# Squares of an RMS norm partly added on GpSimd instead of summed on TensorE: a decoder trunk in fp32

## The chip, the cores and the metric

One core of one Trainium2 chip. The metric is the device time of one launch in microseconds (us), the median of the runs shown.

## The reference, cut to what matters

The kernel computes one inference step of a two-layer decoder trunk for a prompt of 1024 tokens (with 16 learned tokens ahead) and 8 single sample tokens, 1048 token columns in all, in fp32. Layer 0 mixes by retention and a gated linear recurrence, layer 1 by RWKV-7; a gated FFN with a short convolution follows each, and a last norm gives y.

```python
def rms_norm(x, g):
    y = x * lax.rsqrt(jnp.mean(x * x, axis=-1, keepdims=True) + EPS)
    return y * g

x = x + mixer0(rms_norm(x, norm_mix_g[0]))
x = x + conv_ffn(rms_norm(x, norm_ffn_g[0]))
x = x + mixer1(rms_norm(x, norm_mix_g[1]))
x = x + conv_ffn(rms_norm(x, norm_ffn_g[1]))
y = rms_norm(x, norm_final_g)
```

The change touches the mean of x * x in these five norms, over 1024 features.

## The kernel before, in words

Features lie on the partitions and tokens along the free axis. `x` is kept in SBUF as 8 feature tiles (m = 0 to 7) of 128 x 1048, and the tokens are worked in three blocks (`TBS`: 350, 350 and 348 columns). An fp32 product is made of three float32r passes on TensorE (`mm`, L335 to L337): each operand is split in a high part by an ACT copy (L323) and a low part by a VectorE subtraction (L324), both in `split`. Weights come in blocks of 128 x 1024 and are split in the same way.

The program is written in the order in which it is to run, and each engine works off its own instructions in that order. `Weave` runs the dense products as steps and puts side work between them when its share of the time comes up.

An RMS norm of one token block has these parts:

- `norm_sq` (L417): ACT squares one feature tile (L419), into a scratch tile `tmp` (a pool of five) or, at the start, a slot `T`.
- `norm_acc` (L423): TensorE multiplies the squares by a matrix of ones in plain fp32 (L429), so that the sum over the partitions comes out on all of them; eight such sums per block add up in one PSUM bank, `nrm`. With `keep=2` the last two squares stay queued until the next call.
- `norm_scale` (L446 and `rsqrt`, L434 to L437): VectorE takes the mean from PSUM, ACT looks up the inverse root, three VectorE instructions refine it into `rs`.
- `norm_steps`: for each feature tile the emission of h: x times gain times `rs` on VectorE, and the split of the result. The scaling is L479 for the first mixer and both FFNs, L1098 (`norm_emit`) for the RWKV mixer, and L2042 (`fin`) for the last one, where the result is not split but stored.

The norm stands at five places. At the **start**, `layer0` squares and sums block 0 directly; then the squares of the next block alternate with the emission of the block before (`order`, L918 to L925), and its eight sums follow the emission. At the **end of layer 0** and of **both FFNs**, `norm_after` is called behind each step of the product group that completes x (`group_steps` with `tb_outer`: token blocks outside, feature tiles inside). Such a step is six products (two K-tiles), x += product on VectorE (L405, one input in PSUM), a Square, and a sum. After m = 7 of a block its norm is queued as side work behind the steps of the next block. At the end of the recurrence, **before the second FFN**, `finish` (L1934) sums block 0 beside the last output steps and then squares and sums blocks 1 and 2.

Two things hang on the emission after the first FFN. Its first call of `norm_emit` allocates eight slots and starts eight loads of the shift rows (128 x 8) from GpSimd's DMA queue (L1094), and ACT and VectorE split each of them. GpSimd also starts the loads and stores of the FFN's states (L2064, L2066).

Of the kernel before, what the change touches and what calls it, by code (L numbers as in the profile page):

```python
# [29 lines left out]
# ---------------------------------------------------------------- vectors  # L30
# [14 lines left out]
def constants():  # L45
    """Tables that depend on shapes alone."""
# [41 lines left out]
# ---------------------------------------------------------------- host layout  # L88
def cols(v):
    """(..., n*128) -> (128, ..., n): features on partitions."""  # L90
    v = np.asarray(v)
    r = v.reshape(v.shape[:-1] + (v.shape[-1] // 128, 128))
    return np.moveaxis(r, -1, 0)


def wblocks(w):
    """(K, M) -> (M/128, 128, K/128 * 128): one block per 128 output features."""
    k, m = w.shape
    return w.reshape(k // 128, 128, m // 128, 128).transpose(2, 1, 0, 3).reshape(m // 128, 128, k)


def gblocks(w, groups):
    """(K, 1024) cut along K in groups of g tiles -> blocks that hold 8, 4 or 2 output tiles x g K-tiles."""
    out = []
    k0 = 0
    for g in groups:
        a = w[k0 * 128:(k0 + g) * 128].reshape(g, 128, 8, 128).transpose(2, 1, 0, 3)
        n = (8, 4, 2, 2)[g - 1]
        for i in range(0, 8, n):
            out.append(a[i:i + n].transpose(1, 0, 2, 3).reshape(128, n * g * 128))  # L110
        k0 += g
    return out
# [80 lines left out]
# where the parts of a head pair's arithmetic stand beside the next products, in sixths of a 128-wide output tile  # L193
# [9 lines left out]
# K-tiles between stages of which GpSimd takes the lower part  # L203
POOL = (1, 3, 4)

# and of which it takes the mix
MIXP = (4,)

# shares of PE time given to the parts beside the products
L0K = {"start": 0.088, "rope": 0.5, "tr": 1.05, "ret0": 1.312, "ret": 0.35, "lru0": 2.42, "lru1": 2.2, "lru2": 2.2,  # L210
       "lru3": 1.76, "conv": 3.221, "group": 0.748, "wait": 3.6, "norm": 0.845, "norm1": 0.28}
# ---------------------------------------------------------------- device
# [4 lines left out]
class Weave:  # L217
    """Emits dense steps and, between them, side steps as their share of the time comes up."""
# [42 lines left out]

class Prog:
    def __init__(self, tc, io):
        self.tc, self.nc, self.io = tc, tc.nc, io
        self.wq, self.loaded, self.ready = [], [], []
        self.spare, self.nbanks = None, 0
        self.normed, self.sqs, self.nps = set(), [], {}

    # ---- weights: loads two blocks ahead, exact split into two float32r parts one block ahead
# [33 lines left out]
    def scale_w(self, t, kind, j):  # L303
        """Scales a block of w1 | a1 (or g1) by mix (j = 0) or 1 - mix along K."""
# [21 lines left out]
    # ---- one PSUM bank of a product: sum over k of W[k]^T X[k], in three exact float32r passes  # L326
# [21 lines left out]
    # steps of one 128-wide output tile, each token block in so many parts; evac(tb, psum view, c0, c1).  # L348
    # late: the weights of the next tile are not split before this one; pre: they are once its products are out
# [18 lines left out]
    # two tiles side by side at the start of a phase, each token block as soon as its norm is there  # L368
# [6 lines left out]
    # the same tile with the K-tiles outermost: each K-tile of X is done with as early as can be  # L375
# [15 lines left out]
    # steps of x += W^T y over a group of g K-tiles; a weight block holds 8/g output tiles  # L391
# [23 lines left out]
    # ---- RMS norm in parts: squares as the tiles of x become final, the scale per token block, then h  # L415
    def norm_sq(self, m, tb, room=None):
        c0, c1 = TBS[tb]  # L417
        sq = self.tmp(c1 - c0) if room is None else room[:, :c1 - c0]
        self.nc.scalar.activation(out=sq, in_=self.x[:, m, c0:c1], func=AF.Square)  # L419
        self.sqs.append((m, tb, sq))  # L420

    # adds up squares over the features, all but the last few queued
# [8 lines left out]
    def rsqrt(self, y, v, t):  # L431
        """y = v ** -0.5: table value and one Newton step; t is scratch like v."""
# [17 lines left out]
    # emit(m, tb, rs) may return its second half, which then follows the next one's first  # L450
# [14 lines left out]
    # called after each step of the product that completes x: adds up the squares and queues the norm  # L465
# [36 lines left out]
class Layer0:  # L502
# [10 lines left out]
    # ---- retention, head h: q and k with the rotary applied (features on partitions), v by tokens  # L513
# [41 lines left out]
    def dense_ga(self, h, e):  # L555
        """Gate columns of head h: y = silu(g) * (normed o * gain), split as it comes."""
# [14 lines left out]
    # ---- retention core of head h: stages of a chunk one step apart.  # L571
    # All of a chunk's outputs carry gamma^-(c+1), which the group norm takes out again (its eps carries the square).
    def ret_steps(self, h):
# [57 lines left out]
        # chunk 0: the sample rows, each with its own state, and the 16 leading prompt rows  # L631
# [68 lines left out]
        # the stages of a chunk are one step apart  # L700
# [8 lines left out]
    # ---- RG-LRU, one block of 128 features  # L709
# [21 lines left out]
    def lru_steps(self, g):  # L731
        """a = exp(-y) with y = 8 softplus(-lam) r, and sqrt(1 - a^2) = sqrt(t) (1 + a) with t = tanh(y / 2)."""
# [148 lines left out]
def softplus_neg(p, nc, pool):  # L881
    """lamc = 4 softplus(-lam) = 4 (max(-lam, 0) + ln(1 + exp(-|lam|)))."""
# [13 lines left out]
def layer0(p, pool, H, wv):  # L896
# [3 lines left out]
    # norm of the input: the squares of a token block beside the norm of the one before  # L900
# [8 lines left out]
    def sums():  # L909
        for m in range(8):  # L910
            p.norm_sq(m, 0)
            p.norm_acc()
            if m == 5:
                p.prefetch(1)
# [11 lines left out]
    # the tensor engine's clock only rises with use  # L926
# [34 lines left out]
class FFN:  # L961
    """x += W_down^T (gelu(conv(W_ug^T h)) * (W_uv^T h)); f tiles are used in groups of four."""
# [85 lines left out]
class Layer1A:  # L1048
    """RWKV-7, everything up to the recurrence: h, projections, per-chunk decays; results go to scratch in DRAM.

    The decay products inside a chunk of 64 tokens are taken relative to the chunk's 32nd token."""
# [24 lines left out]
    # second-stage low-rank weights have their own queue  # L1076
# [10 lines left out]
    # ---- h of the layer, with the row before each group in front: emitted as x becomes final  # L1087
# [16 lines left out]
    def mix_a(self, n, k, t, pool=False):  # L1104
        """t = (1 - mix_n) h + mix_n h_prev, K-tile k."""
# [11 lines left out]
    def weave(self, steps, side):  # L1117
        """Runs dense steps; side entries (position in sixths of the tile, f) come after the steps before them."""
# [9 lines left out]
    def transition(self, tile, n, temps, side):  # L1128
        """The last tile of a stage with the K-tiles outermost, each K-tile of X replaced by the next stage's after it."""
# [12 lines left out]
    # ---- first stage of the low-rank paths, with the token shift taken after the product:  # L1142
    # evacuation of the product with the shifted weights (j = 0) and with the others (j = 1)
# [36 lines left out]
    def evac_to(self, dst, smp, **act):  # L1180
        """prompt columns to dst[0:1040], sample columns to smp"""
# [13 lines left out]
    # ---- r, and the decays of head pair m relative to the middle of the chunk  # L1195
# [41 lines left out]
    # ---- keys and the per-chunk factors of head pair m  # L1237
# [83 lines left out]
    # sums over the 64 channels of each of two heads, tokens on the partitions: column 2 i + head for the block at HBLK[i]  # L1321
# [7 lines left out]
    # and from there back to all channels of the heads  # L1329
# [16 lines left out]
    def rsq(self, w, y, t):  # L1346
        """t = w ** -0.5 (table value and one Newton step); y is scratch."""
# [6 lines left out]
    def rs_mul(self, v, w, y, t):  # L1354
        """v *= w ** -0.5; y and t are scratch."""
# [11 lines left out]
    # ---- values: by tokens for the recurrence; the gate and the bonus folded into out = yn G1 + G2  # L1367
# [53 lines left out]
    # ---- inverse of I - A on the 32x32 diagonal blocks: forward substitution, one block per partition  # L1421
# [31 lines left out]
    # ---- sample rows: one step of the recurrence each, heads' value rows on the partitions  # L1453
    def samp_pre(self):
# [30 lines left out]
        # rows by sample, then to scratch as (vector, head, sample, key)  # L1485
# [160 lines left out]
class Layer1B:  # L1646
    """RWKV-7 recurrence in chunks of 64 tokens, heads in pairs on the partitions, and the output projection.

    With A = b~ scores, per chunk: U = (I - A_ab)^-1 (a~ S0 + A_ak V), Y = r~ S0 + A_rb U + A_rk V,
    S1 = scale (S0 + b^T U + k^T V). Even heads keep (U, V) rows stacked as U on partitions 0-63 and V on  # L1650
    64-127, odd heads the other way round, so that products over both run on all 128 rows."""
# [45 lines left out]
    # ---- what does not depend on the state: scores, transposed factors, the inverse's lower block  # L1697
# [64 lines left out]
    # ---- the chain  # L1762
# [72 lines left out]
    # ---- group norm over the 64 values of a head, then out = yn G1 + G2  # L1835
# [50 lines left out]
    def run(self, pool):  # L1886
# [15 lines left out]
        for i, u in enumerate(units):  # L1902
# [22 lines left out]
            # a block of tokens is complete one unit after its last chunk  # L1925
# [7 lines left out]
    # the last block of tokens, with the sums for the next norm beside it  # L1933
# [21 lines left out]
def build(tc, io):  # L1955
    nc = tc.nc
    with ExitStack() as ctx:
# [8 lines left out]
        p.rst = pool("rst", 1)  # L1966
        xt = p.x = const.tile([128, 8, T], F32, name="x")
# [5 lines left out]
        with tc.manual_schedule():  # L1973
# [17 lines left out]
            with ExitStack() as cx1:  # L1991
# [10 lines left out]
                with ExitStack() as cx2:  # L2002
# [11 lines left out]
                    # the recurrence's first loads take the place of the layer's X  # L2014
# [70 lines left out]
```

## Time and profile before

| | us |
|---|---|
| median of 3 runs | 3528.8 |
| the runs | 3524.53, 3528.80, 3534.92 |
| span of the profiled execution | 3527.9 |
| TensorE busy | 3305.9 (94%) |
| VectorE busy | 1800.3 (51%) |
| ACT busy | 1241.4 (35%) |
| GpSimd busy | 361.6 (10%) |

The profile is of one execution. Its span runs from the first to the last instruction; no time of its own beside the span is given for it, so it is set against the three runs. Busy times are sums over the whole span, and engines overlap. In rows of the timeline the first number is the start of an instruction (or of a run of like ones) in us from the span's start, the second its length; in brackets is the time its engine sat idle before it, and what ended that. L429 is line 429 of the kernel before.

### The profile page before, as it was taken

Reading aid. Unit: us, or ns where it says so; the run is one execution under the profiler, and the core shown is the slowest. Engines: PE = TensorE matmul, PEld = TensorE weight load, DVE = VectorE, ACT = ScalarE, POOL = GpSimd, SP = SyncE. Lnnn points to the kernel's source line nnn. Section 1 sums busy time; section 2 is a strip of 40 time slices with the busy share of each in tenths; the row PEclk is TensorE's granted clock in tenths of the full one; section 3 lists DMA queues with packets and bytes.
Section 4 is the critical chain, followed back from the end, with each engine's and each line's share of the span. In section 5 each row is a group of like instructions: output and inputs, shape, how many; then the busy total and the mean of one; then the engine's idle time right before and its main releaser. Section 6 shows DMA issues by size and latency. Waiting matters only on the chain.

```text
span 3527.9 us, 55814 instructions
## 1 busy us (share of the span) xinstructions
PE 3305.9 (94%) x23480; PEld 3123.5 (89%) x23480; DVE 1800.3 (51%) x2860; ACT 1241.4 (35%) x2214; POOL 361.6 (10%) x650
## 2 busy tenths in 40 slices
PE   8999999998999999998978978788889999999998
PEld 7999999997999999997978878566767999999997
DVE  4444445556433333334765658677885533333334
ACT  4222224555322212123674444344445312212122
POOL 0110110000000000000111236111210000000000
PEclk9999999999999999999999989678999999999999
DMA  4111211111111111111356768845543111111111
GB/s 134 62 56 60 74 40 46 46 47 34 42 43 48 48 48 42 42 53 48 118 169 169 176 172 232 219 119 143 152 129 96 37 49 46 45 49 42 48 48 64
DMA packets 303066, 294.33 MB, mean 83 GB/s; under 512 B 233056, under 2 KB 248704, under 8 KB 300640
## 3 DMA queue, kind: packets, MB, share of 16 engines
q1 hardware_dynamic: 294368, 262.95, 25.6%
q0 software_dynamic: 8448, 27.82, 2.5%
q8 instruction: 185, 3.03, 0.4%
q14 instruction: 65, 0.53, 0.1%
HBM read 218.95 MB, written 67.47 MB: 81 GB/s over the span
## 4 chain that ended last, share of the span: by engine, by line
PE 29%; DVE 12%; DMA 4%; ACT 3%; issue 3%; SPq 1%; POOL 1%; DVEq 0%; POOLq 0%; ACTq 0%
PE d L337 8%; PE d L335 8%; PE d L336 8%; DVE pr L1439 2%; DVE mt L1441 1%; PE hs L1325 1%; DVE xsl L324 1%; DMA x<-d_pp 1%; DVE wl L324 1%; DMA kq<-d_kq 1%; PE nrm L429 1%; DMA at<-d_ab 1%; DVE x L1213 1%; DVE T L1439 0%; ACT x L1188 0%
## 5 line engine op out<-in xcount | busy, mean ns | idle before, releaser
L335 PE MATMUL d<-xsh,wh 128*128 128x350 f32 (+1 forms) x3656 | 1207.6, 330 | 11.5 <-ACT xsh L323 7.7
L337 PE MATMUL d<-xsl,wh 128*128 128x350 f32 (+1 forms) x3656 | 1193.6, 326 | 5.2 <-DVE xsl L324 5.1
L336 PE MATMUL d<-xsh,wl 128*128 128x350 f32 (+1 forms) x3656 | 1188.0, 325 | 4.4 <-DVE wl L324 4.4
L335 PEld LDWEIGHTS d<-xsh,wh 128*128 128x128 f32 x3656 | 696.2, 190 | 23.2 <-ACT xsh L323 9.3
L337 PEld LDWEIGHTS d<-xsl,wh 128*128 128x128 f32 x3656 | 694.6, 190 | 16.0 <-DVE xsl L324 14.7
L336 PEld LDWEIGHTS d<-xsh,wl 128*128 128x128 f32 x3656 | 696.9, 191 | 7.1 <-DVE wl L324 5.2
L335 PE MATMUL d<-T,wh 128*128 128x350 f32 (+1 forms) x1380 | 463.7, 336 | 15.8 <-DVE x L405 8.9
L324 DVE TENSOR_TENSOR wl<-wst,wh 128x1024 fp32r<-128x1024 f32 x248 | 303.1, 1223 | 320.3 <-ACT wh L323 320.3
L336 PE MATMUL d<-T,wl 128*128 128x350 f32 (+1 forms) x1380 | 445.2, 323 | 2.5 <-DVE wl L324 2.5
L337 PE MATMUL d<-T,wh 128*128 128x350 f32 (+1 forms) x1380 | 445.3, 323 | 1.4 <-DVE T L324 1.4
L323 ACT ACTIVATE wh<-wst 128x1024 fp32r<-128x1024 f32 x248 | 260.7, 1051 | 509.2 <-PE d L337 387.8
L405 DVE TENSOR_TENSOR x<-d,x 128x350 f32<-128x350 f32 (+1 forms) x450 | 230.3, 520 | 322.2 <-PE d L337 322.1
L991 DVE SCALAR_TENSOR_TENSOR T<-T,vec 128x1064 f32<-128x1064 f32 x88 | 116.8, 1327 | 398.2 <-ACT T L989 396.6
L335 PEld LDWEIGHTS d<-T,wh 128*128 128x128 f32 x1380 | 260.0, 188 | 28.2 <-DVE x L405 10.2
L336 PEld LDWEIGHTS d<-T,wl 128*128 128x128 f32 x1380 | 260.1, 188 | 9.9 <-DVE wl L324 3.2
L337 PEld LDWEIGHTS d<-T,wh 128*128 128x128 f32 x1380 | 260.2, 189 | 2.2 <-DVE T L324 2.2
L323 ACT ACTIVATE T<-T 128x1048 fp32r<-128x1048 f32 (+2 forms) x77 | 69.2, 899 | 288.1 <-DVE T L1004 241.2
L985 POOL TENSOR_SCALAR fcout<-T 128x2 f32<-128x2 f32 x44 | 11.2, 254 | 1515.1 <-ACT T L983 1515.1
L983 ACT ACTIVATE T<-d 128x350 f32<-128x350 f32 (+1 forms) x88 | 40.5, 461 | 269.6 <-PE d L337 269.6
L324 DVE TENSOR_TENSOR T<-T 128x1048 fp32r<-128x1048 f32 (+2 forms) x77 | 78.9, 1024 | 76.7 <-ACT T L323 76.7
L1004 DVE TENSOR_TENSOR T<-T,d 128x350 f32<-128x350 f32 x88 | 45.2, 515 | 120.5 <-PE d L337 120.4
L1439 DVE TENSOR_TENSOR pr<-mt,at 128x1 f32<-128x1 f32 (+45 forms) x124 | 93.9, 757 | 19.1 <-DMA at<-d_ab 13.5
(412 smaller groups left out, 4261.4 us busy)
## 6 DMA issues: line engine op xcount, KB each, us to landing
wst<-in_w_up SPq DMA_DIRECT2D x88, 512.0 KB, 3.2
wst<-in_w_down SPq DMA_DIRECT2D x44, 512.0 KB, 3.6
wst<-in_w_in SPq DMA_DIRECT2D x40, 512.0 KB, 3.2
kq<-d_kq SPq DMA_DIRECT2D x17, 1024.0 KB, 6.7
wst<-in_w_o SPq DMA_DIRECT2D x32, 512.0 KB, 4.0
T<-d_sv SPq DMA_DIRECT2D x80, 128.0 KB, 3.8
d_kq<-x SPq DMA_DIRECT2D x16, 544.0 KB, 4.4
d_kq<-x SPq DMA_DIRECT2D x32, 272.0 KB, 5.4
```

The source lines that it names most:

```text
L323: self.nc.scalar.activation(out=h, in_=src, func=AF.Copy)
L324: (eng or self.nc.vector).tensor_tensor(out=l, in0=src, in1=h.bitcast(F32), op=OP.subtract)
L335: mm(ps, lhsT=h, rhs=a, start=start and j == 0, stop=False)
L336: mm(ps, lhsT=l, rhs=a, start=False, stop=False)
L337: mm(ps, lhsT=h, rhs=b, start=False, stop=stop and j == n - 1)
L405: self.nc.vector.tensor_tensor(out=xv, in0=ps, in1=xv, op=OP.add)
L429: self.nc.tensor.matmul(self.nps[tb][:, :n], lhsT=self.ones, rhs=sq, start=m == 0, stop=m == 7)
L983: nc.scalar.activation(out=ub[:, 18 + c0:18 + c1], in_=ps, func=AF.Copy)
L991: nc.vector.scalar_tensor_tensor(out=c, in0=ub[:, j:1064 + j], scalar=w[j], in1=c, op0=OP.mult, op1=OP.add)
L1004: nc.vector.tensor_tensor(out=st["f"][:, c0:c1], in0=c[:, 16 + c0:16 + c1], in1=ps, op=OP.mult)
L1213: nc.vector.tensor_tensor_scan(L, self.rst, s, 0.0, OP.mult, OP.add)
L1439: nc.vector.tensor_tensor(out=pr, in0=mt[:, 0:t, 0:t], in1=at[:, 0:t, t].unsqueeze(1).to_broadcast([n, t, t]), op=OP.mult)
```

## The change

`norm_sq` now writes the square of tile m = 0 into a buffer of its own, `nac` (a new pool `nsp` with one buffer of 128 x 350), and GpSimd adds the squares of m = 1 to 5 onto it. After m = 5 `nac` is queued for TensorE in the place of those six, so that TensorE has three sums per block: `nac`, m = 6 and m = 7. Block 0 of the start (`direct=True`) is as before; the other 14 norms of a block are changed. The squares on ACT and everything on VectorE are the same. Lines behind the new code are up to 15 numbers higher (L429 is L444, L1094 is L1109, L335 is L338; the add is L431).

```diff
+NPOOL = 5
...
-    def norm_sq(self, m, tb, room=None):
+    def norm_sq(self, m, tb, room=None, direct=False):
         c0, c1 = TBS[tb]
-        sq = self.tmp(c1 - c0) if room is None else room[:, :c1 - c0]
+        n = c1 - c0
+        if m == 0 and not direct:
+            sq = self.nac[tb] = self.nsp.tile([128, 350], F32, tag="nac", name="nac")[:, :n]
+        else:
+            sq = self.tmp(n) if room is None else room[:, :n]
         self.nc.scalar.activation(out=sq, in_=self.x[:, m, c0:c1], func=AF.Square)
-        self.sqs.append((m, tb, sq))
+        if not direct and m <= NPOOL:
+            acc = self.nac[tb]
+            if m:
+                self.nc.gpsimd.tensor_tensor(out=acc, in0=acc, in1=sq, op=OP.add)
+            if m == NPOOL:
+                self.sqs.append((0, tb, self.nac.pop(tb)))
+        else:
+            self.sqs.append((m, tb, sq))
...
         for m in range(8):
-            p.norm_sq(m, 0)
+            p.norm_sq(m, 0, direct=True)
             p.norm_acc()
...
         p.rst = pool("rst", 1)
+        p.nsp = pool("nsp", 1)
```

What this does to the order of instructions on an engine is seen at three places.

GpSimd at the end of the first FFN, before (`fcout` is the FFN's state to be stored, `T` the slots of h with the shift rows):

```order
L985 TENSOR_SCALAR fcout<-T 128x2
L986 TENSOR_SCALAR fcout<-T 128x16
L1094 DMA T<-in_st_shift 128x8 x8
L2066 DMA out_fconv<-fcout 128x396
L1064 MEMSET T 128x1088
```

and after:

```order
L1000 TENSOR_SCALAR fcout<-T 128x2
L1001 TENSOR_SCALAR fcout<-T 128x16
L431 TENSOR_TENSOR nac<-nac,tmp 128x350 x8
L1109 DMA T<-in_st_shift 128x8 x8
L431 TENSOR_TENSOR nac<-nac,tmp 128x350 x2
L431 TENSOR_TENSOR nac<-nac,tmp 128x348 x5
L2082 DMA out_fconv<-fcout 128x396
```

The eight loads of the shift rows now stand behind the five adds of the first block and three of the second, and the store of the state behind all 15.

TensorE at the start of layer 0, before, where the first product tile of block 0 ends:

```order
L335 MATMUL d<-xsh,wh 128x350
L336 MATMUL d<-xsh,wl 128x350
L337 MATMUL d<-xsl,wh 128x350
L429 MATMUL nrm<-T,ones 128x350 x8
L335 MATMUL d<-xsh,wh 128x350
```

and after:

```order
L338 MATMUL d<-xsh,wh 128x350
L339 MATMUL d<-xsh,wl 128x350
L340 MATMUL d<-xsl,wh 128x350
L444 MATMUL nrm<-nac,ones 128x350
L444 MATMUL nrm<-T,ones 128x350 x2
L338 MATMUL d<-xsh,wh 128x350
```

Eight sums of the second block have become three, at the same place.

TensorE in the last product group of layer 0, before, around a sum of the first block:

```order
L335 MATMUL rs<-T,wh 128x350
L336 MATMUL rs<-T,wl 128x350
L337 MATMUL rs<-T,wh 128x350
L429 MATMUL nrm<-tmp,ones 128x350
L335 MATMUL d<-T,wh 128x350
L336 MATMUL d<-T,wl 128x350
L337 MATMUL d<-T,wh 128x350
```

and after, where the first sum of that block now stands:

```order
L338 MATMUL rs<-T,wh 128x350
L339 MATMUL rs<-T,wl 128x350
L340 MATMUL rs<-T,wh 128x350
L444 MATMUL nrm<-nac,ones 128x350
L338 MATMUL d<-T,wh 128x350
L339 MATMUL d<-T,wl 128x350
L340 MATMUL d<-T,wh 128x350
```

Before, each step of six products is followed by a sum; now eight steps run without one, then comes that of `nac`, and the other two follow three steps later, ahead of the block's scale.

## Rows read from the trace of the kernel before

**Rows 1.** The page: busy time, share of the span and instructions of each engine

```profile
PE 3305.9 (94%) x23480; PEld 3123.5 (89%) x23480; DVE 1800.3 (51%) x2860; ACT 1241.4 (35%) x2214; POOL 361.6 (10%) x650
```

**Rows 2.** Windows: stretch, length, then PE, PEld, DVE, ACT, POOL busy, PEclk, DMA

```profile
10.00:60.00 50.00, 42.88 (x186) 32.44 (x187) 32.39 (x67) 29.96 (x64) 0.00 (x0) 0.93 0.30 106
...
1620.00:1675.00 55.00, 45.20 (x215) 37.08 (x216) 33.34 (x68) 22.09 (x49) 0.00 (x0) 0.97 0.14 47
...
3465.00:3527.00 62.00, 46.24 (x239) 38.80 (x237) 35.44 (x68) 18.69 (x32) 0.00 (x0) 0.93 0.20 70
```

**Rows 3.** Timeline of TensorE in layer 0's last group, and the chain before the second FFN

```profile
842.40 0.75 PE L429 MATMUL nrm<-tmp,ones 128*128 128x350 f32 x2
...
843.95 0.75 PE L429 MATMUL nrm<-tmp,ones 128*128 128x350 f32 x2
...
2716.46 8.24 PE nrm L429 x28
```

**Rows 4.** Timeline of GpSimd, operations with two inputs in SBUF

```profile
1822.58 2.46 POOL L324 TENSOR_TENSOR xsl<-x,xsh 128x1048 fp32r<-128x1048 f32 x1 [16.16 <-ACT xsh L323]
...
2141.25 1.27 POOL L1520 TENSOR_TENSOR T<-T 128x512 f32<-128x512 f32 x1 [4.20 <-DVE T L1518]
```

**Rows 5.** Timeline of VectorE beside GpSimd, at 1718 to 1727 and at 2141

```profile
1718.66 1.29 DVE L1115 SCALAR_TENSOR_TENSOR x<-T,vec,x 128x1039 f32<-128x1039 f32 x1
...
1720.97 4.87 POOL L324 TENSOR_TENSOR xsl<-T,xsh 128x1048 fp32r<-128x1048 f32 x2 [2.26 <-PE d L337]
...
1721.03 2.42 DVE L1114 SCALAR_TENSOR_TENSOR x<-T,vec,x 128x8 f32<-128x8 f32 x1
1723.38 3.57 DVE L1115 SCALAR_TENSOR_TENSOR x<-T,vec,x 128x1039 f32<-128x1039 f32 x1
1726.87 0.22 DVE L1114 SCALAR_TENSOR_TENSOR x<-T,vec,x 128x8 f32<-128x8 f32 x1
...
2141.80 0.48 DVE L1385 TENSOR_TENSOR x<-hp,T 128x320 f32<-128x320 f32 x1
```

**Rows 6.** Timeline of the start, 22 to 46

```profile
22.54 0.58 DVE L479 SCALAR_TENSOR_TENSOR tmp<-x,vec,rs 128x350 f32<-128x350 f32 x1
...
23.47 0.57 DVE L479 SCALAR_TENSOR_TENSOR tmp<-x,vec,rs 128x350 f32<-128x350 f32 x1
...
29.16 4.87 PE L429 MATMUL nrm<-T,ones 128*128 128x350 f32 x16
...
34.08 0.52 DVE L446 TENSOR_SCALAR tmp<-nrm 128x350 f32<-128x350 f32 x1 [3.58 <-PE nrm L429]
...
45.03 0.59 PE L335 MATMUL d<-xsh,wh 128*128 128x350 f32 x1
```

**Rows 7.** Timeline of VectorE at the end of layer 0

```profile
850.80 0.51 DVE L446 TENSOR_SCALAR tmp<-nrm 128x350 f32<-128x350 f32 x1
...
857.26 0.52 DVE L324 TENSOR_TENSOR xsl<-tmp,xsh 128x350 fp32r<-128x350 f32 x1 [0.52 <-ACT xsh L323]
```

**Rows 8.** The shift rows: timeline of GpSimd and ACT, and the DMA issues

```profile
1606.79 4.28 POOL L1094 DMA_DIRECT2D T<-in_st_shift  x8
...
T<-in_st_shift POOLq DMA_DIRECT2D x8, 4.0 KB, 1.9
...
1645.02 0.88 ACT L323 ACTIVATE xsh<-T 128x8 fp32r<-128x8 f32 x8
```

**Rows 9.** Timeline of ACT in `finish`, before the second FFN

```profile
2717.14 8.07 ACT L419 ACTIVATE tmp<-x 128x350 f32<-128x350 f32 x14 [2.03 <-PE nrm L429]
2725.12 1.04 ACT L323 ACTIVATE wh<-wst 128x1024 fp32r<-128x1024 f32 x1
```

**Rows 10.** Timeline of VectorE at the end of the program

```profile
3497.47 0.52 DVE L405 TENSOR_TENSOR x<-d,x 128x350 f32<-128x350 f32 x1
...
3510.10 0.51 DVE L446 TENSOR_SCALAR tmp<-nrm 128x350 f32<-128x350 f32 x1
```

**Rows 11.** Windows, columns as in rows 2, before the second FFN

```profile
2732.00:2736.00 4.00, 4.00 (x14) 3.48 (x14) 4.00 (x10) 1.99 (x4) 0.00 (x0) 0.50 0.00 0
```

More of the change, by code (lines that the diff above doesn't have):

```diff
@@ L266, in __init__ @@
         self.spare, self.nbanks = None, 0
-        self.normed, self.sqs, self.nps = set(), [], {}
+        self.normed, self.sqs, self.nps, self.nac = set(), [], {}, {}
     def load_next(self):
```

## The prediction

> **What bounds the kernel now.** I read the page's busy times first: TensorE is busy 94% of the span [rows 1]. That is a mean. So I next read the five places where the changed norm runs, in the view of windows: at the start TensorE is busy 42.88 of 50 us, after the first FFN 45.20 of 55, at the end 46.24 of 62, and its granted clock there is 0.93 to 0.97 [rows 2]. TensorE therefore has holes exactly where its sums go. Then the timeline, for prices and for the engine that ends each hole.
>
> An RMS norm makes a chain: sums on TensorE, scale on VectorE (L446), rsqrt, then eight pairs on VectorE (scaling by L479, L1098 or L2042, and the subtraction of `split`), and only then the next products. Where this chain ends last, TensorE time saved beside it is worth nothing.
>
> **What TensorE is rid of.** Of the 120 sums, 70 go (five in each of 14 blocks). In a product group a sum and its six products take 1.55 us (842.40 to 843.95); in the chain of waits 14 sums (28 records) take 8.24 us, 0.59 each [rows 3]. So a step without its sum takes 0.97 us, and 70 x 0.59 = 41 us of TensorE work go. That is the ceiling; the parts below say how little of it lies on the path.
>
> **What GpSimd gets.** 70 adds of 128x350, both inputs in SBUF. No row of before has one. The nearest are adds or subtractions of 512 elements, 1.27 us, and of 1048 elements, 2.46 us [rows 4]: 2.2 ns an element, so about 0.92 us at 350, with a little for the semaphore 0.94; the ends are 0.82 (2.46 in proportion, with no fixed part) and 1.27 us. The Trainium skill (GPSIMD Engine Reference, section 3.1 on elementwise work) times an add of 2048 fp32 elements at 4497 ns, in proportion an estimate of 0.77 us at 350; by it the sum below would be about 3 us smaller.
>
> **What an add does to VectorE.** This term decides. A VectorE instruction with two SBUF inputs takes 1.29 us alone (L1115). Under two GpSimd subtractions that last 4.87 us together, the 8-element L1114 took 2.42 us, where the next one takes 0.22, and L1115 took 3.57 us: each stood until a GpSimd instruction had ended. An operation with one input in PSUM, inside a GpSimd instruction at 2141, took 0.48 us as ever [rows 5]. So x += product (L405) and L446 read PSUM and are free; the scalings, the subtractions and two of the rsqrt's steps have two SBUF inputs and stand for up to a whole add. The Trainium skill (SBUF — State Buffer, "Who interferes with whom") says the same of a VectorE instruction with two SBUF inputs beside a GpSimd one that reads SBUF: whoever starts first holds the shared port pair for its whole instruction. The trace agrees, with 3.57 against 1.29 us, and the rule speaks against this change. Ends: an add costs VectorE nothing, or 0.94 us whole.
>
> **Start (two blocks).** VectorE emits its pairs back to back, 0.93 us a pair (22.54 to 23.47), while ACT squares the next block [rows 6]. Five adds in each of the two emissions cost 5 x 0.94 = 4.7 us each. In the first, eight sums of 4.87 us become three of 1.83, so L446 (34.08) comes 4.7 - 3.0 = 1.7 later. In the second nothing is gained: its sums already stood beside the emission. TensorE's restart at 45.03 moves with it: **+6.4 us**. With adds that cost VectorE nothing it would be -3.0.
>
> **End of layer 0.** The first block's steps are paced by TensorE, so its L446 (850.80) comes earlier by most of 5 x 0.59 = 2.95, say 2.4. From there VectorE's chain paces: a subtraction waits 0.52 us for ACT's half of the split [rows 7], and half of an add fits in that wait. Three adds fall into each emission: 2 x 3 x 0.5 = +3.0. The sum of `nac` stands in TensorE's queue at step m = 7, behind the last add: +0.9. Together **+1.5** (-2.4 to +5).
>
> **End of the first FFN.** The same -2.4, +0.9 and, since VectorE is less loaded [rows 2], +2.4 for the adds. But here a queue is passed. The eight loads of the shift rows (L1094) are issued by GpSimd at 1606.79, 38 us before ACT splits them at 1645.02; they take 4.28 us to issue and 1.9 to land [rows 8]. In the change they stand behind eight adds, the last of which needs the Square of m = 3 in the second block, and that comes at about the time of the split. ACT would then wait for the end of that add, seven more issues (7 x 0.535) and 1.9 us: +5.9 us, with everything queued behind it on ACT, the next Squares and splits. TensorE's cover for that is gone already, since VectorE's chain ends last here. **+6.8** (-2.4 to +9).
>
> **Before the second FFN** (`finish`). Five sums fewer before the last product end (-2.95), but then ACT's Squares, 14 in 8.07 us until 2725.12 [rows 9], are paced by adds through five buffers at about 1.0 us each, and the first Square of a block waits for TensorE's sum of the one `nac` buffer. The weight split behind them comes at about the same time: **0** (-2.9 to +2.5).
>
> **End.** -2.4 up to the first L446. From there to the second, 3497.47 to 3510.10, are 12.6 us [rows 10]; without sums ten steps would take 9.7, and three adds 2.8 more: nothing gained. **-2.4** (-3.5 to 0).
>
> **Clock.** After a hole before the second FFN the granted clock was 0.50, the lower level, for 4 us of full work [rows 11]: 2 us lost, some 2.5 with its edges. The start and the first FFN's end have longer holes in the change; I take one such drop, **+2.5** (0 to 5).
>
> **Sum:** 6.4 + 1.5 + 6.8 + 0 - 2.4 + 2.5 = +14.8 us on the profiled span of 3527.9, thus 3542.7. That span lies 0.9 us below the median of the three runs (3528.8), which vary by more; so 3543 us. About 0.3%, 10.6 us, is what can be told from no change.
>
> **Rivals.**
> 1. *The adds cost VectorE about half*, since many fall into its waits and it starts first: start +1.7, layer 0's end 0, first FFN +5, before the second 0, end -2.9, no drop of the clock: +3.8, 3532 us. For it: the waits of 0.52 us [rows 7]. Against it: at the start there are none.
> 2. *The adds cost VectorE nothing*, and only the late loads remain: -3.0 - 1.5 + 4.4 + 0 - 3.5 = -3.6, 3524 us. Rows 5 speak against it. The point that decides is the scaling at the start: 0.58 us still, or about 1.5.
> 3. *Faster:* as 2, and the loads aren't late, because the wait in `finish` and the shift rows are covered: -3.0 - 1.5 - 1.5 - 2.9 - 3.5 = -12.4, 3515 us. Its mechanism is the shorter step, 0.97 for 1.55 us, reaching every L446. For it: TensorE paces the steps up to the first one. Against it: rows 5 and 8.
> 4. *Worse:* every wait passes whole: start +8, layer 0's end +4, first FFN +9, `finish` +2.5, end -1, two drops +5: +27, 3555 us.
>
> **Chances.** The forecast 0.58, its own range 3537 to 3548, a sixth of it under the bound of 3539.4; rival 1 0.15; rival 2 0.11; rival 3 0.06; rival 4 0.10. So faster 0.06; the same 0.10 + 0.15 + 0.11 = 0.36; slower 0.48 + 0.10 = 0.58. The range reaches from just under rival 2 to rival 4's edge, 3523 to 3556, and leaves out rival 3 and the tails of 2 and 4.
>
> **What would show it.** Adds of about 0.94 us. At the start, pairs of VectorE at 1.87 us where an add falls and 0.93 elsewhere, the L446 of the second block at about 36 and of the third at about 52. After the first FFN, L1109's loads issued after 1640 and an ACT wait of some 5 us for them before the splits of 128x8. At the end, the first L446 some 2 us nearer to the group's start. The forecast is wrong if the scalings stay at 0.58 us under an add, or if ACT never waits for the shift rows; it is wrong in its size if the chain that ends last in those stretches is TensorE's products after all.

## The result, and the profile after

The change is slower: 3551.8 us median (3544.4 to 3557.8, 4 runs) against 3527.8 for the kernel before in the same comparison, a ratio of 1.0067 with an interval of 1.0049 to 1.0085. The span of its profiled execution is 3551.8 us, 23.9 more than before.

The page's first part for the change answers to [rows 1]; TensorE is busy 18 us less, and the span is longer:

```profile
span 3551.8 us, 55689 instructions
...
PE 3288.1 (93%) x23340; PEld 3119.0 (88%) x23340; DVE 1812.8 (51%) x2860; ACT 1242.4 (35%) x2214; POOL 433.8 (12%) x720
```

VectorE carries out the same 2860 instructions in the same order in both kernels. So each can be paired with its twin, and the distance between their starts tells how late the change is at that point. Between two points that distance grew or shrank by (us, against the first trace of before, counted from VectorE's small instructions at 8 us, where the change is 0.6 early; in brackets, a second trace of before against the first):

| place | the change | (before again) |
|---|---|---|
| start, up to 150 us | +8.2 | (+1.2) |
| rest of layer 0, to 830 | -0.5 | (0.0) |
| norm at the end of layer 0 | +4.5 | (0.0) |
| first FFN, 915 to 1590 | +1.4 | (0.0) |
| norm at the end of the first FFN | +4.1 | (+0.1) |
| RWKV mixer, 1705 to 2670 | +0.1 | (-7.7) |
| norm before the second FFN (`finish`) | +1.6 | (+0.8) |
| second FFN, 2770 to 3440 | +4.6 | (0.0) |
| end | +0.2 | (0.0) |

The bracket says what such a table can tell. Outside the RWKV mixer two executions of one kernel agree to about 1 us, in the FFNs to 0.1; inside it they lie 8 us apart, and nothing below rests on that part of a single trace. Across kernels the table is coarser: at norms where an experiment below has the code of before (1, 6 and 9), it still moved by up to 2.2 us, so the +1.6 and +0.2 of the last two norms say little by themselves.

**The start.** Timeline of GpSimd and VectorE of the change, to be held against [rows 6]:

```profile
23.29 1.96 POOL L431 TENSOR_TENSOR nac<-nac,T 128x350 f32<-128x350 f32 x2 [17.85 <-ACT T L427]
25.53 0.93 POOL L431 TENSOR_TENSOR nac<-nac,T 128x350 f32<-128x350 f32 x1 [0.28 <-ACT T L427]
...
23.29 1.18 DVE L494 SCALAR_TENSOR_TENSOR tmp<-x,vec,rs 128x350 f32<-128x350 f32 x1
24.39 1.24 DVE L327 TENSOR_TENSOR xsl<-tmp,xsh 128x350 fp32r<-128x350 f32 x1
25.56 1.28 DVE L494 SCALAR_TENSOR_TENSOR tmp<-x,vec,rs 128x350 f32<-128x350 f32 x1
26.76 0.51 DVE L327 TENSOR_TENSOR xsl<-tmp,xsh 128x350 fp32r<-128x350 f32 x1
...
35.81 0.52 DVE L461 TENSOR_SCALAR tmp<-nrm 128x350 f32<-128x350 f32 x1 [1.24 <-PE nrm L444]
...
51.19 0.52 DVE L461 TENSOR_SCALAR tmp<-nrm 128x348 f32<-128x348 f32 x1 [1.45 <-PE nrm L444]
```

An add takes 0.93 us. Under it a scaling takes 1.18 to 1.28 us where it took 0.58, and a subtraction 1.24 where it takes 0.51; without an add beside them they are as before. An x += that reads PSUM is not held; this one stands inside three adds that run from 876.07 to 879.88, and takes what it takes alone:

```profile
879.03 0.51 DVE L408 TENSOR_TENSOR x<-d,x 128x348 f32<-128x348 f32 x1
```

The second block's scale (L461, once L446) comes at 35.81 and the third's at 51.19. TensorE has less to do meanwhile. The windows (columns as in [rows 2]) show its clock, first before, then the change:

```profile
24.00:28.00 4.00, 3.83 (x15) 2.90 (x14) 4.00 (x10) 3.39 (x9) 0.00 (x0) 0.70 0.00 0
28.00:32.00 4.00, 3.82 (x15) 2.62 (x15) 1.94 (x3) 2.08 (x4) 0.00 (x0) 1.00 0.11 20
```

```profile
24.00:28.00 4.00, 2.40 (x7) 1.51 (x7) 4.00 (x6) 1.96 (x5) 2.21 (x4) 0.50 0.00 0
28.00:32.00 4.00, 3.03 (x10) 2.31 (x10) 4.00 (x7) 2.19 (x6) 1.95 (x2) 0.50 0.00 0
```

PEclk is 0.50, the lower of its two levels, where it was 0.70 and then 1.00.

Not all of the +8.2 belongs to the adds. The first block's scale, ahead of any add, is 1.3 us later than in the first trace of before (counted from 8 us; the second trace of before has 1.2 there). From it to the third block's scale come 5.0 us: each emission loses 3.3, the first one's fewer sums give 2.3 back, and 0.7 go at the sums of the third block. The last 1.9, up to 150 us, come mostly at L543, which waits for a DMA; experiment 6, which has no add at the start, loses 2.1 there too.

**The end of layer 0.** Timeline of the change, and below it a window of before (the same work, some 7 us earlier) and two of the change:

```profile
857.23 0.52 DVE L461 TENSOR_SCALAR tmp<-nrm 128x350 f32<-128x350 f32 x1 [0.72 <-POOL nac L431]
...
883.85 0.92 POOL L431 TENSOR_TENSOR nac<-nac,tmp 128x348 f32<-128x348 f32 x1 [2.66 <-ACT tmp L427]
...
884.81 1.53 PE L444 MATMUL nrm<-nac,ones 128*128 128x348 f32 x2 [6.22 <-POOL nac L431]
...
892.28 0.18 ACT L995 ACTIVATE T<-d 128x8 f32<-128x8 f32 x1 [4.04 <-PE d L340]
...
893.22 0.52 DVE L327 TENSOR_TENSOR xsl<-tmp,xsh 128x350 fp32r<-128x350 f32 x1 [3.66 <-ACT xsh L326]
```

```profile
874.00:878.00 4.00, 3.73 (x21) 3.04 (x20) 3.45 (x8) 2.24 (x4) 0.00 (x0) 1.00 0.09 37
```

```profile
881.00:885.00 4.00, 0.19 (x1) 0.19 (x2) 3.93 (x7) 1.36 (x4) 1.34 (x3) 0.50 0.19 74
885.00:889.00 4.00, 4.00 (x12) 3.51 (x13) 4.00 (x9) 2.33 (x5) 1.08 (x4) 0.50 0.49 137
```

Here is a chain. TensorE stands 6.22 us with the sum of `nac` at the head of its queue, until the last add is done. Its clock is then at the lower level (0.50, where it was 1.00), and the first products of the FFN take 0.29 us each (888.18 to 888.47) in place of 0.16. ACT's evacuation of that product (L995) waits for them and stands ahead of the split of h in ACT's queue. VectorE then waits 3.66 us for that split. By the pairing, 3.7 of the place's 4.5 us arise in this one step. The chain is read from the rows; no run took the wait of the sum away by itself.

**The end of the first FFN.** Timeline of GpSimd and ACT, to be held against [rows 8], and two rows of the waits from 1640 to 1700 (total, times, longest):

```profile
1653.97 0.92 POOL L431 TENSOR_TENSOR nac<-nac,tmp 128x350 f32<-128x350 f32 x1 [3.59 <-ACT tmp L427]
1654.84 4.29 POOL L1109 DMA_DIRECT2D T<-in_st_shift  x8
...
1656.90 0.21 ACT L326 ACTIVATE xsh<-T 128x8 fp32r<-128x8 f32 x1 [3.07 <-DMA T<-in_st_shift]
```

```profile
PE nrm L444 <- POOL nac L431: 21.0, 3, 11.9
...
ACT xsh L326 <- DMA T<-in_st_shift: 5.2, 6, 3.1
```

```profile
1666.01 1.53 PE L444 MATMUL nrm<-nac,ones 128*128 128x350 f32 x2 [11.88 <-POOL nac L431]
```

The loads are issued right behind the eighth add, 48 us later than before, and ACT waits for them. By the pairing VectorE is 8.7 us late at the refined `rs` and 14.5 at the first x += behind the shift rows: 5.8 us in between. Up to the end of the place 2.6 more are added. TensorE stands 11.88 us before a sum of `nac` here, longer than at the end of layer 0; experiment 3 tells how much of the place hangs on the loads.

**The FFNs** hold nothing that the change touches, and yet they lose 1.4 and 4.6 us, evenly over their length. The experiments below show where from.

### The profile page after: what moved, and what is told of

It is laid out like the page before. It is cut to its first block, busy times and chain, and to the rows that moved or that the text cites. A ratio compares the mean times of both kernels' runs of the same rounds, so it can differ in the third digit from the quotient of the medians.

```text
span 3551.8 us, 55689 instructions
## 1 busy us (share of the span) xinstructions
PE 3288.1 (93%) x23340; PEld 3119.0 (88%) x23340; DVE 1812.8 (51%) x2860; ACT 1242.4 (35%) x2214; POOL 433.8 (12%) x720
## 4 chain that ended last, share of the span: by engine, by line
PE 56%; DVE 13%; ACT 4%; issue 4%; DMA 4%; POOL 2%; SPq 1%; DVEq 0%; POOLq 0%; ACTq 0%
PE d L338 17%; PE d L340 17%; PE d L339 17%; DVE pr L1454 2%; PE hs L1340 1%; DVE mt L1456 1%; DMA kq<-d_kq 1%; DVE xsl L327 1%; DVE wl L327 1%; PE gate L776 1%; DMA x<-d_pp 1%; DVE x L408 1%; ACT wh L326 1%; PE rs L340 1%; PE rs L338 1%
## 5 line engine op out<-in xcount | busy, mean ns | idle before, releaser
L338 PE MATMUL d<-xsh,wh 128*128 128x350 f32 (+1 forms) x3656 | 1212.6, 332 | 7.2 <-ACT xsh L326 4.0
L338 PEld LDWEIGHTS d<-xsh,wh 128*128 128x128 f32 x3656 | 698.0, 191 | 18.8 <-issue 7.0
L338 PE MATMUL d<-T,wh 128*128 128x350 f32 (+1 forms) x1380 | 455.9, 330 | 18.3 <-DVE x L408 9.5
L338 PEld LDWEIGHTS d<-T,wh 128*128 128x128 f32 x1380 | 261.8, 190 | 26.1 <-DVE x L408 11.6
L1827 POOL TENSOR_SCALAR s0v<-S 64x256 f32<-64x256 f32 x64 | 66.1, 1032 | 348.6 <-DVE S L1819 212.0
```

The costliest lines, as they stand in the source:

```text
L338: mm(ps, lhsT=h, rhs=a, start=start and j == 0, stop=False)
L1827: nc.gpsimd.tensor_scalar(s0v[r, :, h, :], S[r], 1.0, None, op0=OP.mult)
```

## The experiments

Each experiment is set against runs of before made beside it, so the time of before differs from one comparison to the next. The interval in brackets behind a ratio is the one of 95%; the ratio on record can differ a little from the quotient of the two medians.

**1. The start alone.** Twelve of the fourteen blocks as before:

```diff
-            self.norm_sq(m, tb)
+            self.norm_sq(m, tb, direct=True)
```

(in `norm_after`, and the same in `finish`).

> Only the two blocks at the start use the adds; the other twelve are as before. Theory (adds hold up VectorE's scalings and subtractions there): against the kernel before, VectorE's instructions lie 5 us later at 60 us and 5 to 7.5 us later from 100 us on, and that distance stays constant to the end: about 3534 us. Rival (the loss at the start is noise between runs, or is caught up later): within 2 us of before.

Measured: 3546.2 us against 3523.4, ratio 1.0065 (1.0050 to 1.0080), nearly as much as the whole change. By the pairing the start loses 10.3 us. The rest is where the experiment does nothing: 4.3 in layer 0, 1.4 and 4.6 over the two FFNs. The theory's mechanism is there and its time is far off; something common to the kernels adds to it. (In this trace the RWKV mixer is 9.8 us shorter than in the first trace of before; the other places add up to 21.)

**2. Without the adds.**

```diff
-            if m:
-                self.nc.gpsimd.tensor_tensor(out=acc, in0=acc, in1=sq, op=OP.add)
```

> The 70 adds are left out (the squares of m = 1 to 5 go into no sum); TensorE has three sums per block as in the change. Theory (the adds are the loss: their hold on VectorE, the late shift rows behind them, and the wait of the sum of nac for the last add): the loss of 24 us goes and TensorE's shorter steps come through at four places, 3514 to 3522 us. Rival (the loss comes from TensorE, which waits more and falls to the lower clock level once its sums are gone): 3530 us or more.

Measured: 3522.4 us against 3523.4, ratio 0.9998 (0.9981 to 1.0016). The adds are indeed the cause of most of the loss. At the norms this kernel gains 4.4, 3.3 and 6.2 us at the last three places. The FFNs lose 1.4 and 4.6 us here too, so neither theory has the whole. The start loses 2.7 even without adds. The second block's scale does come 2.9 us earlier, but then TensorE has next to nothing to do, and its clock falls:

```profile
36.00:40.00 4.00, 0.59 (x1) 0.50 (x2) 4.00 (x10) 3.83 (x10) 0.00 (x0) 0.92 0.01 2
40.00:44.00 4.00, 3.67 (x9) 2.25 (x8) 1.87 (x5) 1.37 (x3) 0.00 (x0) 0.50 0.00 0
```

By 55 us 2.2 of the 2.9 are lost again, and from there to 150 us 3.3 more go, mostly at the instruction that waits for a DMA. So at this place the rival has a part.

**3. The shift rows loaded ahead.**

```diff
+            if m == tb == 0:
+                getattr(getattr(emit, '__self__', None), 'shift_rows', lambda: None)()
             self.norm_sq(m, tb)
...
```

The part left out moves the eight slots and their loads from `norm_emit` into a method of their own, `shift_rows`.

> The change, with the eight loads of the shift rows issued ahead of the first add of that norm. Theory (ACT's wait for them goes to the end): ACT waits for no shift row, and 5 to 6.5 us go, to 3545 or 3546 us. Rival (the time passes to TensorE's wait for the sum of nac or to VectorE's chain): less than 2 us go.

Measured: 3545.2 us against 3523.4, ratio 1.0064 (1.0049 to 1.0079), which doesn't stand clear of the change's 1.0067. The trace does: the end of the first FFN goes from +4.1 to -1.3, and ACT goes through all eight splits at once, as it did before:

```profile
1652.34 0.88 ACT L326 ACTIVATE xsh<-T 128x8 fp32r<-128x8 f32 x8
```

So the late loads cost 5.4 us there, as the theory says. The medians are 24.0 and 21.8 us over before, too near each other to tell.

**4. GpSimd busy without reading.**

```diff
-                self.nc.gpsimd.tensor_tensor(out=acc, in0=acc, in1=sq, op=OP.add)
+                for _ in range(3):
+                    self.nc.gpsimd.memset(sq, 0.0)
```

> Each add is replaced by three memsets of its square: GpSimd waits for the same Square and is busy for about as long, but reads nothing in SBUF (the squares of m = 1 to 5 go into no sum). Theory (VectorE is held by GpSimd's reads): the pairs at the start stay at 0.93 us and the time lies above that of the kernel without adds only by the late shift rows, some 5 us: 3519 to 3527 us. Rival (any GpSimd work in SBUF holds VectorE): the start as in the change, and 3540 us or more.

Measured: 3533.9 us against 3523.4, ratio 1.0030 (1.0016 to 1.0045): between the two forecasts. On VectorE the verdict is plain:

```profile
22.70 6.19 POOL L432 MEMSET T<- 128x350 f32 x15 [17.25 <-ACT T L427]
...
22.73 0.58 DVE L495 SCALAR_TENSOR_TENSOR tmp<-x,vec,rs 128x350 f32<-128x350 f32 x1
23.22 0.52 DVE L327 TENSOR_TENSOR xsl<-tmp,xsh 128x350 fp32r<-128x350 f32 x1
23.66 0.57 DVE L495 SCALAR_TENSOR_TENSOR tmp<-x,vec,rs 128x350 f32<-128x350 f32 x1
```

Beside memsets the pairs follow at 0.93 us. What holds VectorE is GpSimd's reading of SBUF, as the Trainium skill has it (SBUF — State Buffer, "Who interferes with whom"), and not its being busy. The loads are late here as in the change: its first FFN's end loses 4.1 us, where the kernel without adds gains 4.4. These 8.5 us, not 5, and 4.2 at the norm before the second FFN, are what lifts the time above that of experiment 2; three memsets take 1.24 us where an add takes 0.93, so GpSimd is also busy for longer than in the change.

**5. Before, once more.**

> The kernel before, unchanged, for a second trace of it. Theory (what the changed kernels' traces show beside the norms, a stall of some 4.6 us in the state updates of layer 0 and a slow loss of some 4.5 us over the second FFN, differs from execution to execution): one or both show up here too. Rival (they belong to the change): this trace agrees with the first one within 2 us all along.

Measured: 3523.5 us (one execution), and the rival is right: both FFNs agree with the first trace to 0.1 us, and so does layer 0. The loss over the FFNs belongs to the changed kernels. (The 4 to 5 us that come or go in the rest of layer 0 in some experiments are a stall around the state updates of retention, L661, that falls to none, one or two of the heads; before has one, at 477 us in both traces. What sets their number stayed open.)

**6. All but the start.**

```diff
-        p.norm_sq(m, tb, room[0][:, m % 3 * 350:m % 3 * 350 + 350])
+        p.norm_sq(m, tb, room[0][:, m % 3 * 350:m % 3 * 350 + 350], direct=True)
```

> The change without the two blocks at the start. Theory (each place loses on its own; by the changed kernel's trace the end of layer 0 loses 4.6 us, the end of the first FFN 4.3, the norm before the second FFN 1.6, the end nothing): 8 to 12 us over before. Rival (the start alone is the whole loss, which the run with the start alone suggests with its 22.8 us): within 5 us of before.

Measured: 3548.0 us against 3526.7, ratio 1.0062 (1.0047 to 1.0077). The two halves cost 22.8 and 21.2 us and the whole 24: they don't add up, so a part of the loss is in each of them once. Of the 20 us counted twice, 6 are those over the FFNs; 4.3 in experiment 1 are the stall named under 5; the rest was not found. Again the FFNs lose 1.4 and 4.7.

**7. The first blocks alone** (at the four places other than the start).

```diff
-            self.norm_sq(m, tb)
+            self.norm_sq(m, tb, direct=tb > 0)
```

(in `norm_after`; in `finish` blocks 1 and 2, and at the start all blocks, are as before.)

> Adds for the first token block alone, at the four places other than the start: there VectorE only adds products from PSUM, no emission runs yet, and no shift row is loaded behind the adds. Theory (adds cost nothing where VectorE has no instruction with two SBUF inputs, and the first L446 comes earlier): 2.4 us less at three places and 2.9 before the second FFN, together 5 to 10 us under before, some 3515 us. Rival (what TensorE saves there, it waits for elsewhere): within 3 us of before.

Measured: 3532.8 us against 3526.7, ratio 1.0014 (1.0003 to 1.0025): neither. At the end of the first FFN it gains 3.1, before the second 1.4, at the end 1.3, at the end of layer 0 nothing (+0.4); and the FFNs lose 1.4 and 4.6.

**8. Three adds in place of five.**

```diff
-NPOOL = 5
+NPOOL = 3
```

> The change with the squares of m = 0 to 3 in nac, so three adds and five sums a block. Theory (the loss goes with the adds that hold VectorE and with the wait for the last of them): TensorE waits for nac for less than half as long, the pairs at the start lose 2.8 us an emission at most, and 8 to 14 us over before are left. Rival (the loss comes with the change of place at all, whatever the number of adds): 20 us or more over before.

Measured: 3543.5 us, 16.7 over before, ratio 1.0047 (1.0034 to 1.0060). TensorE waits 5.9 us for `nac` at the end of layer 0 (10.5 in the change) and 9.4 at the first FFN's end (21.0); the start loses 1.6. The loss shrinks with the adds, by less than expected. The FFNs' share stays, and the end of the first FFN loses 5.5 us, more than the change's 4.1, since the loads stand behind adds here too.

**9. The room of `nac` alone.** What all these kernels share is the new pool. Its 1400 bytes, rounded to 1408 by the program's allocations, push every later SBUF buffer further on, among them the FFNs' slots `T` and, in the second FFN, its h, which TensorE reads.

```diff
         p.rst = pool("rst", 1)
+        pool("nsp", 1).tile([128, 350], F32, tag="nac", name="nac")
```

> The kernel before with the room of nac reserved in SBUF and never used: the same instructions, but everything that is allocated behind it lies 1408 bytes further on. In every changed kernel so far, the one with the start alone among them, TensorE's products in the second FFN stand 159.8 ns apart, in both traces of before 158.7. Theory (the place in SBUF sets this): 159.8 ns here too, 1 us later over the first FFN and 4 to 5 us over the second, 4 to 8 us over before. Rival (the instructions, not the place): 158.7 ns, no difference to before.

Measured: 3535.5 us against 3528.6, ratio 1.0025 (1.0013 to 1.0037), with the instructions of before. The windows from 2900 to 3200 us count TensorE's products, first before, then the second trace of before, the change, and the room alone:

```profile
2900.00:3200.00 300.00, 300.00 (x1893) 300.00 (x1892) 102.94 (x138) 70.01 (x90) 6.23 (x36) 1.00 0.14 46
```

```profile
2900.00:3200.00 300.00, 300.00 (x1892) 300.00 (x1892) 103.29 (x137) 70.01 (x90) 6.23 (x36) 1.00 0.15 46
```

```profile
2900.00:3200.00 300.00, 300.00 (x1879) 300.00 (x1878) 104.20 (x143) 64.98 (x82) 5.53 (x32) 1.00 0.15 46
```

```profile
2900.00:3200.00 300.00, 300.00 (x1879) 300.00 (x1878) 102.67 (x137) 68.69 (x88) 6.22 (x36) 1.00 0.15 46
```

TensorE is never idle, its clock is 1.00 in all four, and it gets through 1893 products or 1879: 0.7% fewer where the buffers have moved by 1408 bytes. By the pairing the two FFNs lose 1.4 and 4.6 us here as well. The theory holds.

**10. The change with 2048 bytes for `nac`.**

```diff
-            sq = self.nac[tb] = self.nsp.tile([128, 350], F32, tag="nac", name="nac")[:, :n]
+            sq = self.nac[tb] = self.nsp.tile([128, 512], F32, tag="nac", name="nac")[:, :n]
```

> The whole change, with 2048 bytes for nac in the place of 1400, so that what lies behind it moves by 2048 and not by 1408 bytes. Theory (place): 158.7 ns in the second FFN, and 4 to 7 us less than the change, 17 to 20 us over before. Rival (the instructions): 159.8 ns, 24 us over before.

Measured: 3542.9 us against 3528.6, ratio 1.0045 (1.0029 to 1.0062), 14.3 us over before. The interval, 10 to 22 us, overlaps that of the change (17 to 30), so the pairing is what tells them apart: both FFNs lose nothing (0.0 and 0.0), and the count is that of before:

```profile
2900.00:3200.00 300.00, 300.00 (x1893) 300.00 (x1892) 101.91 (x138) 67.15 (x87) 6.22 (x36) 1.00 0.15 46
```

What is left at the places of the norms is +8.4, +3.2, +4.1, +1.3 and +2.5.

**11 and 12. The first blocks alone, with 2048 and with 1536 bytes for `nac`.** Edits 7 and 10 together, with `[128, 512]` and `[128, 384]`.

> Adds for the first token block alone at the four places other than the start, as in the earlier run that came out some 5 us over before, with 2048 bytes for nac. Theory (that run lost by the place what its shorter steps gained): 1 to 6 us under before. Rival (the shorter steps gain nothing): as before or slower.

> The same as the first blocks alone with 2048 bytes for nac, but with 1536 bytes, a multiple of 512 and not of 1024. Theory (a move by a multiple of 512 bytes keeps TensorE's pace): 158.7 ns in the second FFN, 0 to 6 us under before. Rival (it takes a larger multiple): 159 ns or more there, and a time over before.

Measured: 3524.9 us against 3528.6, ratio 0.9994 (0.9981 to 1.0007); and 3521.2 against 3528.0, ratio 0.9984 (0.9969 to 0.9998). Both have the pace of before in the second FFN (1893 products), so a move by a multiple of 512 bytes is enough here. (1408 is a multiple of 128, so that alone is not; 256 was not tried.) For 1536 bytes:

```profile
2900.00:3200.00 300.00, 300.00 (x1893) 300.00 (x1892) 103.79 (x138) 70.18 (x91) 6.25 (x36) 1.00 0.15 46
```

The last of them is the fastest of all kernels run, by 0.16%, with an interval that only just leaves out no difference. That the idea of the change gave this is not shown. The four norms' places together gain 5.0 us in the trace with 2048 bytes and lose 0.7 in the one with 1536. Both traces gain 5 us in the rest of layer 0, where the stall named under 5 does not occur. The end of the first FFN differs most, -3.1 against +0.6, and there the clock differs, first with 2048 bytes, then with 1536:

```profile
1624.00:1628.00 4.00, 3.64 (x20) 2.92 (x19) 1.51 (x3) 1.32 (x4) 3.92 (x8) 1.00 0.36 119
```

```profile
1624.00:1628.00 4.00, 4.00 (x15) 4.00 (x15) 1.05 (x2) 0.99 (x2) 1.09 (x2) 0.50 0.37 128
```

As far as these two traces tell, some 4 us at that place hang on the clock of the one execution.

## Why the prediction was right, point by point

The forecast was 3543 us, slower, and the range reached to 3556; 3551.8 came. Its sign, and the chance that it gave to slower, rest on a mechanism that the runs show. The size was short by 9 us: 6 of them over the FFNs, of which the sum had no term; the terms at the norms' places, 14.8 in sum, came to 18.6 by the pairing.

- *What an add does to VectorE*: shown, by the change's rows at the start and by the memsets of experiment 4. The price of an add, 0.94, was 0.93. The cost to VectorE was put at a whole add; the five adds of an emission cost it 3.3 us, not 4.7. Two adds back to back took 1.96 and 2.13 us, more than twice 0.93, so an add waits for VectorE too; why a part of each add is not lost was not tried. (All three of the rsqrt's VectorE steps have two SBUF inputs, not two of them as the prediction has it.)
- *Start*, +6.4: +8.2, and partly by luck. The L446 that were forecast at about 36 and 52 came at 35.81 and 51.19, but 0.75 us of either was there before the first add; from the first scale on they came 1.0 and 5.0 later, where 1.7 and 6.4 had been reckoned. The rest of the +8.2 is what lay ahead of the adds and the wait for a DMA behind them.
- *Clock*, +2.5 for one drop: it fell to 0.50 at both of the places that the term named (the start, and 1660 to 1668, where before it was 1.00) and at the end of layer 0. What each drop cost was not measured by itself; it is within the places' numbers.
- *End of layer 0*, +1.5: +4.5. The first scale's gain was there, but smaller: the x += ahead of it came 1.5 us earlier, its L461 only 0.6, since it writes a `tmp` buffer that an add had still to read (VectorE waits 0.72 us for GpSimd there); the refinement behind it came 1.3 earlier. The step that failed is the sum of `nac`, put at 0.9 us of delay: TensorE stood 6.22 us behind it, and the drop of the clock that followed was priced for other places.
- *End of the first FFN*, +6.8: +4.1. ACT's wait for the shift rows came as forecast (5.2 us; 5.8 on VectorE's chain, 5.9 had been reckoned), and loading them ahead took away 5.4. The gain ahead of it, 2.4, was larger: 13.0 us late at 1590, the change was 9.4 late at the first L461 and 8.7 at the refined `rs`. The 3.3 reckoned for the adds and the sum of `nac` came to 2.6.
- *Before the second FFN*, 0: +1.6. As reckoned, the last product end came nearer (by 1.9 us, not 2.95) and ACT lost it again. The second and third blocks' Squares waited 1.69 and 4.10 us for TensorE's sum of the one `nac`:

```profile
2732.37 0.50 ACT L427 ACTIVATE nac<-x 128x350 f32<-128x350 f32 x1 [1.69 <-PE nrm L444]
...
2739.88 0.49 ACT L427 ACTIVATE nac<-x 128x348 f32<-128x348 f32 x1 [4.10 <-PE nrm L444]
```

- *End*, -2.4: +0.2. The first L461 was held up by its buffer here too (0.6 gained, and 1.3 at the refinement, not 2.4), and the adds of the next two blocks took that back.
- *Left out*: the place of the new pool in SBUF, 1.4 and 4.6 us over the two FFNs. No term of the sum looked at what the change moves without touching it. Without it (experiment 10) the change costs 14.3 us (10 to 22), where the sum said 14.8; with terms that were off in both directions, so near an agreement is partly luck.

Of the rivals, the one in which the adds cost VectorE nothing fell with the change's rows at the start. The one in which they cost half was as near in that price as the forecast (3.3 us lie about midway between half of 4.7 and the whole), but had no drop of the clock, and nothing for the end of layer 0. The fast one was tried as experiment 2: its places gained as much as had been reckoned, or more, from the first FFN's end on, but the FFNs took 6 us back, and the start's gain came (2.9 us) and was lost again. Not tried were a second `nac` buffer and a sum of `nac` queued behind the other two.

## What to carry to other kernels

Before work goes to GpSimd, look at what VectorE does beside it: instructions with two SBUF inputs stand for most of each GpSimd read (here 3.3 of 4.7 us), those with one input in PSUM do not. Ask of each product that now reads a GpSimd result what stands behind it in TensorE's queue, and of each DMA queue what has been put ahead of it. And compare the pace of stages that the change does not touch: a new buffer in the middle of SBUF moved the rest and cost a quarter of the loss, which sizes of 1536 and 2048 bytes took away. Before a gain of a few us at one place of one trace is believed, look at the clock there in a second trace.

## What the runs showed of the hardware that was not expected

TensorE's pace on float32r products hangs on where its operands lie in SBUF. Moving the later buffers, and with them the moving operand, by 1408 bytes, while the split weights (their pools are allocated ahead) stayed, took it from 1893 to 1879 products in 300 us at the full granted clock; moving them by 1536 or 2048 bytes did nothing. Which pair of accesses gets in each other's way was not tried. Of two executions of one kernel all parts but the RWKV mixer agreed to about 1 us, and the mixer lay 7.7 us apart.
